# ConvFFN up: two plain pairs of blocks in the place of three, and the second half's residual rows issued behind the factor sums

## The chip, the cores and the metric

The kernel runs on one core of a Trainium2 chip. The metric is the device time of one execution in microseconds; the kernel before has a median of 817.88 us over three runs. Engines are named as in the profile: PE (TensorE, the matrix engine), PEld (its weight loads), DVE (VectorE), ACT (ScalarE), POOL (GpSimd) and SP (SyncE, which here only issues DMAs).

## What is computed

A decoder block over 512 tokens of 1024 channels: two causal token mixers, a gated merge, a residual and LayerNorm, then a ConvFFN with another residual and LayerNorm. The change touches the seam between the first LayerNorm and the first half of the ConvFFN:

```python
mix = mixed @ w_out[l]
x = layer_norm(ALPHA * x + mix, ln1_g[l], ln1_b[l])

z = x @ w_ffn_in[l]                       # 1024 -> 2 x 2816
u, gv = jnp.split(z, [D_FF], axis=-1)
u = causal_dwconv(u, w_ffn_dw[l], b_ffn_dw[l])
y_ffn = (jax.nn.gelu(u) * gv) @ w_ffn_out[l]
x = layer_norm(ALPHA * x + y_ffn, ln2_g[l], ln2_b[l])
```

## The kernel before

Every product of matrices is made of three matmuls: each operand is split into a high part, rounded by a cast on ACT, and a low part, the rest, by a subtraction on DVE (`split`, L166). `mm3` (L173) then adds high by high, high by low and low by high in PSUM.

ConvFFN up has 22 pairs of blocks, j = 0 to 21. A pair is a block of 128 columns of u and the matching block of the gate branch. It is computed in one of two ways.

A plain pair is two blocks, each over the whole depth of 8 slices of 128. The first `NF` pairs are plain and run together in `up` (L996): first all their blocks for the first half of the tokens (256), then all for the second half. So PE has work while the second half of the tokens is still in LayerNorm 1. `up` calls `pump` ahead of every second slice of the depth. Each call takes one entry from `steps`: an empty step, or a call that traces the transposes and activations of one token block for one half of the depth (`ln1_transposes`, L927). `SP` (L17) gives the number of empty steps ahead of each of the four token blocks: 9 for block 2, 3 for block 3.

A seven-product pair (`seven`, L690) is a 2 x 2 block product done with seven products of half the depth and half the tokens in the place of eight. It needs sums of the weights (`weight_sums`, L659: loads two tiles d and e, forms t13 and t24, and splits b21, then b11 with b22, t1 with t3, t2 with t4) and sums of the activations (`factor_sums`, L940: for each of two token blocks of a half four sums, each one split; most are made in place, on top of an input). Its first product is b11 by a11 into the bank X, then b21 by a12 into W, t1 by s1 into Z, then t2 by s2 into X again. The seventh is left to the following pair (`finish`).

Tiles of the same tag share memory: a new tile waits until the old one's last reader is done. The weights' high and low parts take turns in two rings of five tiles (tags hi and lo). `ring_pair` (L648) places every fifth pair elsewhere, in two extra tiles, where the caller gives some:

```python
if more is not None and ring_n[0] % 5 == 4:
    out.append(p1p.tile([P, 1024], F32R, tag=more, name=f"s{tag}_{key}"))
```

The gates call it 8 x 3 times without extra tiles, so the count is 24 at the first seven-product pair. For ConvFFN up the extra tags are oh2 and oh3. The same tags hold x1[2] and x1[3], the normalised rows of token blocks 2 and 3 (L896). `residual` (L892) multiplies such rows by gamma and adds beta on DVE, in place, and stores them through SP's queue; they are loaded again for the second LayerNorm. For blocks 2 and 3 these calls are collected in `late` and traced when j is `NF`, right after `prepare` of that pair.

The order of instructions on each engine is decided when the program is built: a planner goes by the order in which the code traces them and by when it expects each to be ready. An instruction that is ready early can so be issued ahead of ones that were traced before it. `tc.issue_after(i)` forces what is traced inside it, as far as it is on i's engine, to be issued behind i.

Of the kernel before, what the change touches and what calls it, by code (L numbers as in the profile page):

```python
# [10 lines left out]
F32R = mybir.dt.float32r  # L11
BF16 = mybir.dt.bfloat16
WARM = 7
PLAIN = 3
NF = 3
PLAINS = tuple(range(PLAIN))
SP = (6, 0, 9, 3)  # L17
I32 = mybir.dt.int32
AF = mybir.ActivationFunctionType
ALU = mybir.AluOpType  # L20
# [48 lines left out]
def hybrid_block(ctx: ExitStack, tc: tile.TileContext, wts: bass.AP, xT_d: bass.AP,  # L69
# [3 lines left out]
    ve, ac, po, pe = nc.vector, nc.scalar, nc.gpsimd, nc.tensor  # L73
# [25 lines left out]
    def limit(i):  # L99
        return min(e for e in (W_G, W_FI + 2 * PLAIN, W_S) if e > i) - 1  # L100

# [58 lines left out]
    def weight(i):  # L160
        while state[0] <= min(i + AHEAD, limit(i)):
            fetch(state[0])
            state[0] += 1
        return loaded.pop(i)

    def split(hi, lo, src, hi_eng=None, lo_eng=None):  # L166
        if hi_eng is None:
            ac.copy(hi, src)  # L168
        else:
            hi_eng.tensor_copy(hi, src)  # L170
        (lo_eng or ve).tensor_tensor(lo, src, hi, ALU.subtract)  # L171

    def mm3(ps, a, b, start, stop, more=False):  # L173

# [213 lines left out]
    def cln_channels(j):  # L388
        ps = bank(7 if j else 6)
        for tb in range(NT):  # L390
            pe.transpose(ps[:, tb * P:tb * P + P], cn[tb][:, j * P:j * P + P], ident)
        g, b = pcol(PC_CG + j), pcol(PC_CBETA + j)
        sg = tmp.tile([P, T], F32, tag="t0", name=f"cls{j}", bufs=3)
        y = tmp.tile([P, T], F32, tag="t1", name=f"cly{j}")
        ac.activation(sg, ps, AF.Sigmoid, bias=b, scale=g)  # L395
        ac.activation(y, ps, AF.Identity, bias=b, scale=g)  # L396
        ve.tensor_tensor(y, y, sg, ALU.mult)
        split(ch[:, j], cl[:, j], y)
# [432 lines left out]
    def fo_sums(n, behind):  # L831

        fo = lambda t, m: wts[W_FO + FO_OF[t] + m]
        c, m = divmod(n, 4)
        t, b, a = (("t1", "b12", fo("b11", m)), ("t2", "b22", tsum["t1"][m]), ("t3", "b12", fo("b22", m)),
                   ("t4", "b21", tsum["t2"][m]))[c]

        po.dma_start(tsum[t][m][0:1, 0:16], behind[0:1, 0:16])
        po.dma_start(tsum[t][m], fo(b, m))
        po.dma_start(tsum[t][m], a, accum_op=ALU.add, max_dma_last_dim=4096)  # L840
# [20 lines left out]
    for m in range(NH, KD):  # L861
# [5 lines left out]
        t = tmp.tile([P, T], F32, tag="t0", name=f"gm{m}", bufs=3)  # L867
# [55 lines left out]

    keep = {}
    late = []

    def ln1_transposes(half, tb, n):  # L927
        pt = bank(obk[half][2 * (tb % 2) + n])
        for k in range(4):
            pe.transpose(pt[:, k * P:k * P + P], x1[tb][:, (4 * n + k) * P:(4 * n + k + 1) * P], ident)  # L930
        t = tmp.tile([P, T], F32, tag=("kt", "kT")[n] if half == 0 else ("tot", "t1")[n], name=f"a{half}{n}_{tb}")

        for k in range(4):
            ks = slice(k * P, k * P + P)
            ac.activation(t[:, ks], pt[:, ks], AF.Identity, bias=pcol(PC_L1B + 4 * n + k), scale=pcol(PC_L1G + 4 * n + k))
        dst = (slice(None), half, slice(4 * n, 4 * n + 4), slice((tb % 2) * P, (tb % 2) * P + P))
        split(x1h[dst], x1l[dst], t.rearrange("p (k t) -> p k t", k=4))
        keep[half, n, tb % 2] = t

    def factor_sums(i, sh, sl):  # L940

        a11, a12, a21, a22 = keep[0, 0, i], keep[0, 1, i], keep[1, 0, i], keep[1, 1, i]
        dst = lambda t, n: t[n][:, :, i * P:i * P + P]
        four = lambda t: t.rearrange("p (k t) -> p k t", k=4)

        def emit(n, t):
            split(dst(sh, n), dst(sl, n), four(t))
        ve.tensor_tensor(a22, a21, a22, ALU.add)
        emit(0, a22)
        ve.tensor_tensor(a22, a22, a11, ALU.subtract)  # L950
        emit(1, a22)
        ve.tensor_tensor(a11, a21, a11, ALU.subtract)
        emit(2, a11)
        ve.tensor_tensor(a12, a12, a22, ALU.subtract)
        emit(3, a12)
# [27 lines left out]
    def hid(part):  # L983

        for tag, c0, n in ([("ch", 0, 4), ("cl", 4, 4)], [(f"sc{i}", 8 + 2 * i, 2) for i in range(4)])[part]:
            t_ = p1p.tile([P, n, T], F32, tag=tag, name=f"hT{tag}")
            for c in range(n):
                hT[c0 + c] = t_[:, c]
            for c in range(0, n, 2):
                hT2.append(t_[:, c:c + 2])  # L990
        for c in range(16, NFF) if part else ():
            hT[c] = tmp.tile([P, T], F32, tag=("tot", "kt", "gg")[(c - 16) // 2], name=f"hT{c}")
# [3 lines left out]
    def up(ws, halves):  # L996
        pss = [cring.get() for _ in ws]
        for hf in halves:
            for ps, w in zip(pss, ws):
                for k in range(KD):  # L1000
                    if k % 2 == 0:
                        pump()
                    ks = slice(k * P, k * P + P)
                    if hf is None:
                        dst, x = ps.rearrange("p (a t) -> p a t", a=2), (x1h[:, :, k], x1l[:, :, k])
                    else:
                        dst, x = ps[:, hf * 256:hf * 256 + 256], (x1h[:, hf, k], x1l[:, hf, k])
                    mm3(dst, (w[0][:, ks], w[1][:, ks]), x, k == 0, k == KD - 1)
            while steps:
                pump()  # L1010
        return pss

    def act(j, u, g):
        a = tmp.tile([P, T], F32, tag="t0", name=f"fa{j}", bufs=3)
        w = [pcol(PC_FW + 3 * j + i) for i in range(3)]
        ac.activation(a, u, AF.Identity, bias=pcol(PC_FB + j), scale=w[2])
        ve.scalar_tensor_tensor(a[:, 1:], u[:, 0:T - 1], w[1], a[:, 1:], ALU.mult, ALU.add)
        ve.scalar_tensor_tensor(a[:, 2:], u[:, 0:T - 2], w[0], a[:, 2:], ALU.mult, ALU.add)
        ac.activation(a, a, AF.Gelu_apprx_tanh)
        ve.tensor_tensor(hT[j], a, g, ALU.mult)  # L1020

    def seven_up(j, w, sh, sl):

        a11, a12, a22 = [(x1h[:, h, 4 * n:4 * n + 4], x1l[:, h, 4 * n:4 * n + 4]) for h, n in ((0, 0), (0, 1), (1, 1))]
        pc = tmp.tile([P, 3, 256], F32, tag="mv", name=f"pc{j}", bufs=1)
        ug = tmp.tile([P, 2, T], F32, tag="qq", name=f"ug{j}")

        def last(X):
            urgent(ac.copy, ug[:, 0, 256:512], X)
            act(j, ug[:, 0], ug[:, 1])  # L1030
        seven(cring, 5, w, (a11, a12, a22), list(zip(sh, sl)), pc, ug, last)

    def prepare(j):
        i = W_FI + 2 * j
        if j in PLAINS:
            if state[0] <= i:
                assert state[0] == i
                fetch(i)
                fetch(i + 1)
                state[0] += 2  # L1040
            return [loaded.pop(i), loaded.pop(i + 1)]
        t = [p1p.tile([P, 1024], F32, tag=tag, name=f"T{tag}_{j}") for tag in ("oh0", "oh1")]
        b21 = [tmp.tile([P, T], F32R, tag=tag, name=f"b{tag}_{j}") for tag in ("kT", "t1")]
        return weight_sums(i, t, b21, ("oh2", "oh3"))

    resident[W_FI + 2 * NF - 2] = lambda: tuple(p1p.tile([P, 1024], F32R, tag=f"sc{i}", name=f"fir{i}") for i in range(2))
    fir = p1p.tile([P, 2, 1024], F32R, tag="cl", name="fir")
    resident[W_FI + 2 * NF - 1] = lambda: (fir[:, 0], fir[:, 1])
    first = [weight(W_FI + i) for i in range(2 * NF)]
    pss = up(first, (0, 1))  # L1050
    sht = p1p.tile([P, 4, 4, 256], F32R, tag="ol", name="sh")
    sh = [sht[:, n] for n in range(4)]
    sl = [p1p.tile([P, 4, 256], F32R, tag=f"sv{n}", name=f"sl{n}") for n in range(4)]
    for i in range(2):
        factor_sums(i, sh, sl)
    hid(0)
    for j in range(NF):
        act(j, *pss[2 * j:2 * j + 2])
    assert state[0] == W_FI + 2 * PLAIN, state

    for j in range(NF, NFF):
        if NF + 1 <= j <= NF + 12:
            fo_sums(j - NF + 3, hT[j - 2])
        if j == NF:
            w = prepare(j)
            for f in late:
                f()
            hid(1)
        wn = prepare(j + 1) if j + 1 < NFF else None
        if j in PLAINS:  # L1070
            if pending:
                pending.pop()()
            act(j, *[up([t], (None,))[0] for t in w])
        else:
            seven_up(j, w, sh, sl)
        w = wn
# [23 lines left out]
    four = lambda *tags: [lambda k, t=t: p1p.tile([P, 2, 2, 256], F32R, tag=t, name=f"so{t}_{k}") for t in tags]  # L1100
# [54 lines left out]
    for n, t in enumerate(FOP):  # L1155
        nxt = None
        load_rest(n, ops[0][0][:, 0, 0:1])
        for m in range(4):
# [3 lines left out]
            for c in range(2):  # L1162
                first, end = m == 0 and c == 0, m == 3 and c == 1
                for i in range(2):
# [7 lines left out]
                    hi, lo = (o[:, c, i * P:i * P + P] for o in ops[m])  # L1172
# [114 lines left out]
```

## Time and profile before

| | us |
|---|---|
| median of 3 runs (817.06 to 818.1) | 817.88 |
| the profiled execution | 817.08 |
| its span, first to last instruction | 815.2 |
| PE busy | 803.5 |
| DVE busy | 654.1 |
| ACT busy | 478.5 |

The profiled execution's own time is 1.9 us longer than its span; a difference in the span is taken as the same difference in the time. A busy share is a mean over the whole kernel. What counts here is the seam between 469 and 530 us, where PE goes from the W_out product through the plain pairs to the seven-product pairs, and there the rows of single instructions say more than the shares. Matmuls overlap, so the cost of one is the distance between two starts and not its duration; on DVE too the next instruction starts a little ahead of the listed end of the one before.

### The profile page before, as it was taken

To read this page: it belongs to the slowest core of one execution; us is meant where nothing else is said; L and a number is where in the kernel's file an instruction comes from. 1 tells how busy PE (TensorE), PEld (TensorE's weight loads), DVE (VectorE), ACT (ScalarE), POOL (GpSimd) and SP (SyncE) were. 2 spreads that over 40 slices of the span, in tenths; PEclk is the share of its full clock that TensorE was granted. 3 is DMA by queue.
4 is the path that set the end of the run, shared out by engine and by line. 5 is a ranking of instruction groups with operands and counts; after the bars stand their busy time and mean duration, and the time that the engine had idled before them with its cause. 6 is when DMAs were issued, how large, how long until landed. Compare 5 with 4: busy or idle time off the path is not lost.

```text
span 815.2 us, 14709 instructions
## 1 busy us (share of the span) xinstructions
PE 803.5 (99%) x5723; PEld 711.6 (87%) x5723; DVE 654.1 (80%) x1158; ACT 478.5 (59%) x856; POOL 111.0 (14%) x194
## 2 busy tenths in 40 slices
PE   9999999999999999999999999999999999999995
PEld 6888778888888788999988899999999999888884
DVE  5598687888877649788474899899898999999566
ACT  5356657576779865566741657466666666776400
POOL 0012331333323200001200000011111100000000
PEclk9999999999999999999999999999999999999998
DMA  8569876756545663466885322467676753777502
GB/s 305 173 142 246 205 162 149 184 130 155 140 121 133 141 180 114 115 175 171 199 281 227 107 100 80 136 181 203 181 205 194 192 161 116 253 238 229 171 26 78
DMA packets 38534, 136.50 MB, mean 167 GB/s; under 512 B 4928, under 2 KB 5824, under 8 KB 38208
## 3 DMA queue, kind: packets, MB, share of 16 engines
q1 hardware_dynamic: 27072, 90.98, 33.2%
q0 software_dynamic: 9952, 40.90, 24.4%
q10 hardware_dynamic: 1440, 3.68, 1.2%
q8 instruction: 45, 0.74, 0.4%
q14 instruction: 25, 0.20, 0.1%
HBM read 108.28 MB, written 20.97 MB: 159 GB/s over the span
## 4 chain that ended last, share of the span: by engine, by line
PE 96%; ACT 1%; DVE 1%; DMA 0%; issue 0%; DVEq 0%
PE ps L175 30%; PE ps L177 30%; PE ps L176 30%; PE ps L443 1%; PE ps L599 1%; PE ps L588 1%; PE ps L561 1%; PE ps L601 1%; PE ps L615 1%; PE ps L930 0%; PE ps L578 0%; DMA xr<-in_xT 0%; ACT cls L395 0%; ACT cly L396 0%; PE ps L379 0%; DVE x1a L1211 0%
## 5 line engine op out<-in xcount | busy, mean ns | idle before, releaser
L175 PE MATMUL ps<-xh,wh 128*128 128x512 f32 x256 | 102.7, 402 | 0.3 <-ACT xh L168 0.3
L177 PE MATMUL ps<-xh,wl 128*128 128x512 f32 x256 | 100.1, 391 | 0.0
L176 PE MATMUL ps<-xl,wh 128*128 128x512 f32 x256 | 99.9, 390 | 0.0
L302 DVE SCALAR_TENSOR_TENSOR cws<-cws,par 128x512 f32<-128x512 f32 x120 | 86.3, 761 | 1.0
L156 ACT CAST wh<-wr 128x1024 fp32r<-128x1024 f32 (+1 forms) x50 | 50.4, 1013 | 57.2 <-PE ps L177 38.5
L157 DVE TENSOR_TENSOR wl<-wr,wh 128x1024 fp32r<-128x1024 f32 (+1 forms) x51 | 58.9, 1162 | 20.0 <-ACT wh L156 19.5
L143 ACT CAST wh<-wr 128x1024 fp32r<-128x1024 f32 x44 | 46.3, 1053 | 41.9 <-PE ps L176 34.2
L175 PE MATMUL ps<-sh,shi_t 128*128 128x256 f32 x228 | 64.5, 283 | 0.0
L176 PE MATMUL ps<-sl,shi_t 128*128 128x256 f32 x228 | 64.5, 283 | 0.0
L177 PE MATMUL ps<-sh,slo_t 128*128 128x256 f32 x228 | 64.5, 283 | 0.0
L175 PEld LDWEIGHTS ps<-xh,wh 128*128 128x128 f32 x256 | 48.1, 188 | 11.1 <-ACT xh L168 1.2
L145 POOL DMA_DIRECT2D wl<-wr x44 | 38.5, 882 | 137.3 <-ACT wl L144 95.5
L177 PEld LDWEIGHTS ps<-xh,wl 128*128 128x128 f32 x256 | 48.0, 188 | 10.3
L171 DVE TENSOR_TENSOR slo_t<-Toh,shi_t 128x1024 fp32r<-128x1024 f32 x38 | 46.5, 1223 | 12.7 <-ACT shi_t L168 12.7
L176 PEld LDWEIGHTS ps<-xl,wh 128*128 128x128 f32 x256 | 48.2, 188 | 9.5 <-DVE xl L171 0.4
L168 ACT CAST shi_t<-Toh 128x1024 fp32r<-128x1024 f32 x38 | 39.5, 1047 | 14.8 <-PE ps L176 13.0
L144 ACT ACTIVATE wl<-wh 128x1024 fp32r<-128x1024 f32 x44 | 46.5, 1059 | 0.5
L293 ACT COPY pc<-ps 128x256 f32<-128x256 f32 x57 | 21.2, 372 | 41.7 <-PE ps L177 41.2
L175 PEld LDWEIGHTS ps<-sh,shi_t 128*128 128x128 f32 x228 | 43.8, 192 | 0.0
L176 PEld LDWEIGHTS ps<-sl,shi_t 128*128 128x128 f32 x228 | 43.8, 192 | 0.0
L177 PEld LDWEIGHTS ps<-sh,slo_t 128*128 128x128 f32 x228 | 43.8, 192 | 0.0
L171 DVE TENSOR_TENSOR slo_b<-wr,shi_b 128x1024 fp32r<-128x1024 f32 x27 | 33.0, 1223 | 2.4 <-ACT shi_b L168 2.4
(465 smaller groups left out, 2574.5 us busy)
## 6 DMA issues: line engine op xcount, KB each, us to landing
wr<-in_wts SPq DMA_DIRECT2D x137, 512.0 KB, 4.3
wl<-wr POOLq DMA_DIRECT2D x44, 512.0 KB, 5.1
t<-in_wts POOLq DMA_DIRECT2D x24, 512.0 KB, 4.9
wr<-t SPq DMA_DIRECT2D x16, 512.0 KB, 4.2
t<-t POOLq DMA_DIRECT2D x8, 512.0 KB, 6.8
x<-in_x ACTq DMA_DIRECT2D x4, 512.0 KB, 9.5
x_d<-x SPq DMA_DIRECT2D x4, 512.0 KB, 2.8
x1a<-x_d SPq DMA_DIRECT2D x4, 512.0 KB, 3.6
```

The costliest lines, as they stand in the source:

```text
L143: ac.copy(hi, raw)
L144: ac.mul(lo, hi, -1.0)
L145: po.dma_start(lo, raw, accum_op=ALU.add)
L156: ac.copy(hi[:, c], raw[:, c])
L157: ve.tensor_tensor(lo[:, c], raw[:, c], hi[:, c], ALU.subtract)
L168: ac.copy(hi, src)
L171: (lo_eng or ve).tensor_tensor(lo, src, hi, ALU.subtract)
L175: pe.matmul(ps, a[0], b[0], start=start, stop=False, skip_group_check=more)
L176: pe.matmul(ps, a[0], b[1], start=False, stop=False, skip_group_check=more)
L177: pe.matmul(ps, a[1], b[0], start=False, stop=stop, skip_group_check=more)
L293: f(*args)
L302: ve.scalar_tensor_tensor(cacc[j], cpad[j][:, i:i + T], w, cacc[j], ALU.mult, ALU.add)
```

## The change

`PLAIN` and `NF` go from 3 to 2. Pairs 0 and 1 are plain and run together in `up`, so four blocks and not six; pair 2 is computed by seven products, and its weights are packed for that in DRAM. The tiles apart from the ring that held the weights of pair 2 now hold those of pair 1. `SP` stays as it is.

`split` returns its subtraction, and `factor_sums` keeps the last one in `made`. The residual rows of token blocks 2 and 3 are traced at the same place as before, but their DVE operations are to be issued behind the last subtraction of the factor sums.

```diff
--- before.py
+++ after.py
@@ -11,8 +11,8 @@
 F32R = mybir.dt.float32r
 BF16 = mybir.dt.bfloat16
 WARM = 7
-PLAIN = 3
-NF = 3
+PLAIN = 2
+NF = 2
 PLAINS = tuple(range(PLAIN))
 SP = (6, 0, 9, 3)
 I32 = mybir.dt.int32
@@ -168,7 +168,7 @@
             ac.copy(hi, src)
         else:
             hi_eng.tensor_copy(hi, src)
-        (lo_eng or ve).tensor_tensor(lo, src, hi, ALU.subtract)
+        return (lo_eng or ve).tensor_tensor(lo, src, hi, ALU.subtract)
 
     def mm3(ps, a, b, start, stop, more=False):
 
@@ -923,6 +923,7 @@
 
     keep = {}
     late = []
+    made = []
 
     def ln1_transposes(half, tb, n):
         pt = bank(obk[half][2 * (tb % 2) + n])
@@ -944,7 +945,7 @@
         four = lambda t: t.rearrange("p (k t) -> p k t", k=4)
 
         def emit(n, t):
-            split(dst(sh, n), dst(sl, n), four(t))
+            made[:] = [split(dst(sh, n), dst(sl, n), four(t))]
         ve.tensor_tensor(a22, a21, a22, ALU.add)
         emit(0, a22)
         ve.tensor_tensor(a22, a22, a11, ALU.subtract)
@@ -1063,8 +1064,10 @@
             fo_sums(j - NF + 3, hT[j - 2])
         if j == NF:
             w = prepare(j)
-            for f in late:
-                f()
+
+            with tc.issue_after(made[0].ins):
+                for f in late:
+                    f()
             hid(1)
         wn = prepare(j + 1) if j + 1 < NFF else None
         if j in PLAINS:
```

## Rows read from the trace of the kernel before

**Rows 1.** The page's busy time of each engine (busy us, share of the span, instructions), and below it the view of what PE waited for over the whole execution (engine, line, tile, releaser: us in total, times, longest).
```profile
PE 803.5 (99%) x5723; PEld 711.6 (87%) x5723; DVE 654.1 (80%) x1158; ACT 478.5 (59%) x856; POOL 111.0 (14%) x194
...
PE ps L615 <- ACT cly L396: 1.3, 1, 1.3
PE ps L113 <- DVE wrs L109: 1.2, 1, 1.2
PE ps L175 <- ACT xh L168: 0.3, 1, 0.3
```

**Rows 2.** PE's timeline through ConvFFN up (start in us, duration in us, line, operation, out<-in, how many were merged): the first matmul on the normalised activations, the transposes of token blocks 2 and 3, the first matmul of the fifth plain block, the first matmul of the second half of the tokens, and the first product of three seven-product pairs in a row.
```profile
469.46 0.28 PE L175 MATMUL ps<-x1h,wh 128*128 128x256 f32 x1
...
477.74 1.03 PE L930 MATMUL ps<-ident,x 128*128 128x128 f32 x8
...
480.40 0.60 PE L930 MATMUL ps<-ident,x 128*128 128x128 f32 x4
...
481.56 0.60 PE L930 MATMUL ps<-ident,x 128*128 128x128 f32 x4
...
482.71 0.28 PE L175 MATMUL ps<-x1h,fir 128*128 128x256 f32 x1
...
488.47 0.28 PE L175 MATMUL ps<-x1h,wh 128*128 128x256 f32 x1
...
505.75 0.28 PE L175 MATMUL ps<-x1h,shi_b 128*128 128x256 f32 x1
...
514.39 0.28 PE L175 MATMUL ps<-x1h,shi_b 128*128 128x256 f32 x1
...
524.47 0.28 PE L175 MATMUL ps<-x1h,shi_b 128*128 128x256 f32 x1
```

**Rows 3.** DVE's timeline in the same stretch, same columns: three pieces of weight work inside the LayerNorm chain, the residual rows of blocks 2 and 3 (L893, L894), two of the x1l subtractions, the first operation of the factor sums, the subtraction for the first seven-product pair's b11 and b22, and the last subtraction of the factor sums.
```profile
473.69 1.17 DVE L157 TENSOR_TENSOR fir<-wr,fir 128x1024 fp32r<-128x1024 f32 x1
...
474.91 0.68 DVE L681 TENSOR_TENSOR Toh<-wr,Toh 128x512 f32<-128x512 f32 x1
...
475.65 0.68 DVE L682 TENSOR_TENSOR Toh<-wr,Toh 128x512 f32<-128x512 f32 x1
...
478.95 1.22 DVE L893 TENSOR_TENSOR x<-x,gb 128x1024 f32<-128x1024 f32 x1
...
481.83 1.22 DVE L894 TENSOR_TENSOR x<-x,gb 128x1024 f32<-128x1024 f32 x1
...
483.56 1.22 DVE L893 TENSOR_TENSOR x<-x,gb 128x1024 f32<-128x1024 f32 x1
484.70 0.69 DVE L171 TENSOR_TENSOR x1l<-a,x1h 128x512 fp32r<-128x512 f32 x1
485.30 0.69 DVE L948 TENSOR_TENSOR a<-a,a 128x512 f32<-128x512 f32 x1
485.90 1.22 DVE L894 TENSOR_TENSOR x<-x,gb 128x1024 f32<-128x1024 f32 x1
487.04 0.69 DVE L171 TENSOR_TENSOR x1l<-a,x1h 128x512 fp32r<-128x512 f32 x1
...
493.18 1.22 DVE L171 TENSOR_TENSOR slo_b<-wr,shi_b 128x1024 fp32r<-128x1024 f32 x1
...
499.24 0.69 DVE L171 TENSOR_TENSOR sl<-a,sh 128x512 fp32r<-128x512 f32 x1
```

**Rows 4.** ACT's timeline, same columns (in brackets: idle time before and what released it): the first activation of token block 2, the casts of block 3's halves of the depth, and the cast of b11 and b22.
```profile
478.37 1.85 ACT L935 ACTIVATE a<-ps,par 128x128 f32<-128x128 f32 x5 [7.67 <-PE ps L930]
...
483.88 0.68 ACT L168 CAST x1h<-a 128x512 fp32r<-128x512 f32 x1
...
485.65 0.62 ACT L168 CAST x1h<-a 128x512 fp32r<-128x512 f32 x1
...
486.70 1.04 ACT L168 CAST shi_b<-wr 128x1024 fp32r<-128x1024 f32 x1
```

**Rows 5.** Busy time by stretch (from:to in us, length, then busy us and instructions of PE, PEld, DVE, ACT, POOL, then PE's granted clock, the DMA engines' share, GB/s): the stretch around the first seven-product pair, ten pairs behind it, and two stretches at the kernel's tail.
```profile
478.90:513.00 34.10, 34.10 (x287) 34.10 (x287) 34.07 (x47) 25.50 (x46) 1.05 (x2) 1.00 0.28 93
...
515.80:616.00 100.20, 100.20 (x837) 100.20 (x836) 90.10 (x117) 62.05 (x99) 14.44 (x24) 1.00 0.68 184
...
805.00:810.00 5.00, 1.37 (x7) 0.79 (x5) 3.54 (x10) 0.00 (x0) 0.00 (x0) 1.00 0.21 80
810.00:815.00 5.00, 0.00 (x0) 0.00 (x0) 2.02 (x6) 0.00 (x0) 0.00 (x0) 0.54 0.27 105
```

**Rows 6.** SP's timeline (the issues of DMAs) in the same stretch, merged: the stores of blocks 2 and 3 and the next weight loads. Below it, of the view of the store's line, the time from issue to landing of its four stores.
```profile
483.07 4.41 SPq L895 DMA_DIRECT2D x_d<-x  x2
494.50 5.23 SPq L666 DMA_DIRECT2D wr<-in_wts  x2
...
DMA to landing us min/median/max: 2.6/2.8/3.2
```

**Rows 7.** The last matmul on the first pair's b22 in PE's timeline, and in ACT's timeline the cast that comes behind it.
```profile
512.83 0.28 PE L177 MATMUL ps<-sh,slo_b 128*128 128x256 f32 x1
...
513.03 1.05 ACT L168 CAST shi_t<-Toh 128x1024 fp32r<-128x1024 f32 x1 [0.95 <-DVE soat_b L171]
```

## The prediction

> **What bounds the kernel now.** I read the page's busy shares first, then what TensorE (PE) waited for. PE is busy 803.5 of 815.2 us, and its waits sum to under 3 us, all outside ConvFFN up [rows 1]. So a saved matmul is saved time, as long as nothing new makes PE wait. Next I read PE's timeline over the stage that is changed, for its rate and its boundaries [rows 2]: the second half of the W_out product ends at 469.46, the six plain blocks (three pairs, first half of the tokens) run to 488.47, their second half to 505.75, and there the first pair by seven products starts. From 482.71 to 488.47 is 5.76 us for 48 matmuls, so a matmul of 256 columns costs 0.12 us. The seven-product pairs repeat at the same rate: first product at 514.39, the next pair's at 524.47, 10.08 us = 84 x 0.12. Then VectorE (DVE) and ScalarE (ACT) in the same stretch [rows 3, 4]: after PE has finished W_out, the last two token blocks still go through LayerNorm 1, transposes, four ACT passes each, a cast and a subtraction. Last, busy times by stretch [rows 5]: DVE is busy 34.07 of 34.10 us between 478.9 and 513.0, and 90.1 of 100.2 in the pairs after. PE hides all that, but only just in this stretch.
>
> **What the change saves.** A plain pair in halves is 2 blocks x 8 x 3 x 2 = 96 matmuls, 96 x 0.12 = 11.52 us; by seven products it is 7 x 4 x 3 = 84, 10.08 us. Sum: -1.44 us of PE. Everything else of the pair is on other engines. Two subtractions of plain weights (1.17 to 1.22 us each) go from DVE; one full-width and two half-width sums, three full-width subtractions, a half-width one and two sums of products come, some 8.1 us busy for 2.4, so +5.7 us of DVE. Over the later pairs that is hidden in DVE's idle tenth [rows 5]; if it were not, it would cost at most those 5.7 us. The GpSimd sums for the down projection begin one pair earlier and wait for hT[1] in the place of hT[2]; GpSimd is busy 111 of 815 us [rows 1], cost nothing.
>
> **First gap: the second half of the plain blocks.** A matmul of that half needs the activations of token blocks 2 and 3 together. With four plain blocks, the first half is 96 matmuls and the 16 transposes among them, and it ends where block five begins today: 482.71 [rows 2]. The last input for k = 0 to 3 is the cast that starts at 483.88 and lasts 0.68, and the subtraction behind it, which takes 0.69 [rows 3, 4]. Without the residual rows ahead of it on DVE that subtraction runs at 484.6 to 485.2. Today blocks five and six are the cover: the half starts at 488.47, with everything ready at 487.7. Now PE stands from 482.8 to about 485.2: +2.4 us. Moving the residual rows can't shorten this much, since ACT's chain from 478.37 to 486.27 is without a break [rows 4]. Lower bound 0.1: DVE does three pieces of weight work inside the LayerNorm chain (473.69, 474.91, 475.65; 2.3 us together [rows 3]), and if the new order puts them elsewhere the chain ends so much sooner. Upper bound 3.6: with fewer plain weights a ring slot is free early, so one more subtraction of weights (1.2 us) can slip into that chain. I take 2.4, since the same three pieces are due in the same place. Once n = 0 is there, its 48 matmuls (5.76 us) cover the other half of the depth, which ACT finishes at 486.3.
>
> **Second gap: the first seven-product pair.** Its first operand pair (b11 with b22) doesn't lie in the ring but in tiles oh2 and oh3: ring_pair takes the extra tags when its count is 4 modulo 5, and the gates leave it at 24. Those tiles hold x1[2] and x1[3], the rows that the late residual writes and stores. So cast and subtraction of b wait for the two stores. Today the residual rows run at 478.95 to 487.0 as filler [rows 3], the stores issue at 483.07 and 487.2 and land in 2.8 us [rows 6], the cast of b is at 486.70 and its subtraction at 493.18, 11 us before its use at 505.75. That the extra tiles really gate is seen one turn later: the cast that takes them next stands at 513.03, right behind the last matmul on the first b at 512.83 [rows 7].
>
> The change puts all four residual operations behind the last subtraction of the factor sums. Today that one starts at 499.24. Without three residual operations and the 1.2 us for b between them, I put its end at 497.5; bounds 495.4 (some 15 operations at the pitch of 0.60 us between the starts at 484.70, 485.30 and 485.90 [rows 3], behind ACT's last cast at 486.3, nothing between) and 499.9 (as today). Then: four operations at the pitch of 1.14 between 483.56 and 484.70, 4.6; the activation of the second plain pair, traced ahead of them, comes between for 0 to 2.0; the store's landing 2.8 [rows 6]; the subtraction 1.2. So b is whole 8.6 to 10.6 us after the sums; I take 9.0: at 506.5, bounds 504.0 to 510.5.
>
> PE by then: the second half ends at 485.2 + 11.5 = 496.7. Then the two products that need no b (b21 by a12, t1 by s1, 24 matmuls) last to 499.6. From there X can't go on: its first product is b11. The next pair can: its b lies in the ring, and its first three products are another 36 matmuls, 4.3 us, to 503.9; the fourth needs t2, whose ring turn is the same extra tiles. So the gap is 506.5 - 503.9 = 2.6 us if the issue order brings the next pair forward, and 506.5 - 499.6 = 6.9 if not; bounds 0 and 10.9. PE's order here is decided when the program is built, by what is expected to be ready: the first transposes of block 2 stand behind 69 matmuls of the plain blocks, at 477.74, where the code emits them ahead of the 55th (nine empty steps of six matmuls) [rows 2]. So I take the reordered case, 2.6.
> The Trainium skill (TensorE: Matmul & The Clock Gate, section "Step-by-step: what each phase is for") says that the engine pulls weight loads ahead but that matmuls stay in program order. By that a wait for b would hold all behind it, and the sum would be the 6.9; the row shows that the order written may already differ from the code's, so I give that less weight.
>
> **Queues behind the moved step.** Behind the residual rows on DVE stand the weights of the next pair; DVE is full here, so they come as PE's spare products need them, and that is inside the bound. On SP's queue the two stores move from 483 and 487 to some 500 and 503. Behind them are the loads for the pair after next, which wait for the subtraction of b anyway (today at 494.50, right behind 493.18 [rows 3, 6]); at 507 + 3.5 us they still land some 9 us before that pair starts at about 520. Cost nothing; if that cover is gone, the pair waits for the difference.
>
> **The sum.** -1.44 + 2.4 + 2.6 = +3.6 us on the profiled execution: 817.08 + 3.6 = 820.7. That execution lies 0.8 below the median of the runs, 817.88, so the median should come out at 821.5.
>
> **Rivals.**
> First, and on the other side, no gap at all: with the residual rows gone from the front of DVE's queue and the three fillers out of the LayerNorm chain, what PE needs comes before PE does. It decides from the point where the last x1l subtraction for k = 0 to 3 ends by 482.8 in place of 485.2, and b is whole by 499.6, which the fill by the next pair can put off to 503.9. For it: 4.6 us less on DVE ahead of the sums. Against: ACT's unbroken chain. -1.44 gives 816.4.
> Second, the first gap alone: the second is covered because the sums end at 495.4 and no activation comes between. Total +1.0, with the filler +2.2: 818.9 to 820.1.
> Third, slower by more: the order keeps first_x of the first seven-product pair in its place, and all of PE waits for the stores. It decides from the point where the planner expects b before it expects the next pair's operands. -1.44 + 2.4 + 6.9 = +7.9, 825.8. For it: DVE has no free time to prepare the next pair. Against: the displaced transposes [rows 2].
> Fourth, the change doesn't do what it says: the residual rows would have come behind the sums anyway. Against: today they stand ahead of the sums [rows 3].
> The clock is no rival for the first gap: in the tail, a stretch with PE idle for 3.6 us still has the granted clock at 1.00, the 2.4 GHz level, and it is the next stretch that shows 0.54 [rows 5].
>
> **How the numbers follow.** Forecast (both gaps, next pair brought forward; +1.6 to +5.5) 0.45; first gap alone 0.20; no bringing forward 0.20; no gap 0.12; the rest 0.03. Likeliest time 821.5. About 0.2%, 1.6 us, is what a measurement of this kernel can tell from no change. Faster by that (below 816.2): the lower part of the no-gap case and of the rest, 0.08. Within it (816.2 to 819.5): the other part of the no-gap case, half of the first-gap case, the edge of the forecast, 0.25. Slower: 0.67. The range from 816.4 to 826.0 leaves out about half of the case without bringing forward and a part of the no-gap case.
>
> **What would show it.** In the changed profile: PE's waits list a gap of 2 to 3 us ahead of the first matmul on the second half, released by the x1h cast or the x1l subtraction; both residual stores after the sums' last subtraction; cast and subtraction of the first b behind those stores; and a second PE wait on that subtraction, with products of the next pair before it. The pairs after repeat at 10.08 us. The prediction is wrong if PE has no idle time between 480 and 510, if b is prepared before the sums end, or if DVE falls behind for many pairs, which would show as waits on slo_t far beyond 520.

## The result, and the profile after

| | us | ratio to before |
|---|---|---|
| before, median of 4 runs (817.06 to 818.73) | 817.99 | |
| after, median of 4 runs (827.75 to 830.03) | 829.09 | 1.0137 [1.0124, 1.015] |
| predicted | 821.5 (816.4 to 826.0) | |

The change costs 11 us where some 4 were forecast, and the time lies outside the range. The profiled execution of after took 830.03 us, 12.95 more than that of before.

Read first, on the page of after, the busy times (engine, busy us, share, instructions).
```profile
PE 808.1 (98%) x5711; PEld 714.3 (86%) x5711; DVE 659.6 (80%) x1165; ACT 481.6 (58%) x862; POOL 111.2 (13%) x194
```
Then the view of what PE waited for in after (engine, line, tile, releaser: us in total, times, longest). bkT and bt are the tiles of b21's high and low part, shi_b and slo_b those of b11 with b22, shi_t and slo_t those of the t operands; pc holds copies of finished products.
```profile
PE ps L175 <- ACT x1h L168: 1.8, 1, 1.8
PE ps L177 <- DVE bt L171: 1.8, 1, 1.8
PE ps L175 <- ACT shi_b L168: 1.4, 1, 1.4
...
PE ps L175 <- ACT shi_t L168: 1.1, 1, 1.1
PE ps L175 <- ACT pc L293: 1.0, 1, 1.0
PE ps L177 <- DVE slo_b L171: 0.8, 1, 0.8
```
PE has 12 matmuls less than in [rows 1], which is 12 x 0.12 = 1.44 us, and yet is busy 4.6 us longer. So besides the six new waits, 7.9 us together, there are matmuls that became slower. DVE has 5.5 us more of work; 5.7 were worked out.

PE's timeline of after shows where (start, duration, operation, how many merged, in brackets the wait and its releaser): the transposes of block 3, the last first-half matmul before the gap, the first of the second half, two later ones, the first of the first seven-product pair, and the first after each wait.
```profile
482.00 1.09 PE L931 MATMUL ps<-ident,x 128*128 128x128 f32 x8 [0.17 <-DVE x L884]
...
483.05 0.28 PE L177 MATMUL ps<-x1h,fir 128*128 128x256 f32 x1
485.11 0.95 PE L175 MATMUL ps<-x1h,wh 128*128 128x256 f32 x3 [1.78 <-ACT x1h L168]
...
486.07 0.41 PE L176 MATMUL ps<-x1l,wh 128*128 128x256 f32 x1
486.28 0.41 PE L177 MATMUL ps<-x1h,wl 128*128 128x256 f32 x1
...
498.22 0.28 PE L175 MATMUL ps<-x1h,bkT 128*128 128x256 f32 x1
...
500.86 0.39 PE L177 MATMUL ps<-x1h,bt 128*128 128x256 f32 x1 [1.76 <-DVE bt L171]
501.08 0.28 PE L175 MATMUL ps<-x1h,bkT 128*128 128x256 f32 x1
...
506.21 0.58 PE L175 MATMUL ps<-x1h,shi_b 128*128 128x256 f32 x1 [1.41 <-ACT shi_b L168]
...
514.56 0.39 PE L177 MATMUL ps<-x1h,slo_b 128*128 128x256 f32 x1 [0.83 <-DVE slo_b L171]
...
522.60 0.38 PE L175 MATMUL ps<-sh,shi_t 128*128 128x256 f32 x1 [1.05 <-ACT shi_t L168]
```
Two places lose time. At the boundary of the halves the first half ends at 483.17, 0.4 late, since block 3's rows came later; PE then stands to 485.11 (1.94); and the 96 matmuls of the second half take 498.22 - 485.11 = 13.11 us in the place of 11.52 (1.59). Together 3.9 us. The seam behind it is not one gap: from 498.22 to 554.54, where the wait for pc ends, there are 384 matmuls, 46.1 us of work in 56.3, so 10.2 us are lost, in five waits (6.05 us with pc's) and in slow matmuls around them. With the 1.44 saved, 3.9 + 10.2 - 1.4 = 12.7 of the 12.95 us are placed.

The slow matmuls are seen in the pitch, 486.28 - 486.07 = 0.21 us where it was 0.12, and in the busy times by stretch of after (columns PE, PEld, DVE, ACT, POOL busy, then the granted clock, the DMA share and GB/s).
```profile
482.80:485.30 2.50, 0.72 (x6) 0.52 (x5) 1.85 (x4) 2.50 (x8) 0.00 (x0) 0.98 0.00 0
485.30:500.00 14.70, 13.79 (x102) 13.59 (x102) 12.90 (x21) 11.86 (x20) 0.00 (x0) 0.89 0.00 1
500.00:505.00 5.00, 3.94 (x22) 3.65 (x22) 5.00 (x7) 1.63 (x4) 0.53 (x1) 0.73 0.33 105
505.00:510.00 5.00, 3.79 (x21) 3.79 (x22) 5.00 (x6) 2.21 (x3) 0.52 (x1) 0.59 0.90 269
510.00:515.00 5.00, 4.17 (x35) 3.96 (x34) 3.49 (x4) 0.62 (x1) 0.85 (x1) 1.00 0.93 303
```
The granted clock falls behind the wait that ends at 485.11 and again behind the one that ends at 500.86, to means of 0.89, 0.73 and 0.59, that is to the 1.2 GHz level for a part of each stretch. Behind the three shorter waits from 514.56 on it stays at 1.00. Before it was 1.00 throughout [rows 5].

DVE's timeline of after, the pieces that answer to [rows 3] (slo_t, slo_b, bt and L670 are weights of seven-product pairs, L884 the normalised rows of block 3, L1018 an activation of the plain pairs, L893 and L894 the residual rows):
```profile
477.67 1.22 DVE L171 TENSOR_TENSOR slo_t<-Toh,shi_t 128x1024 fp32r<-128x1024 f32 x1
...
479.27 1.23 DVE L670 TENSOR_TENSOR Toh<-wr,wr 128x1024 f32<-128x1024 f32 x1 [0.19 <-DMA wr<-in_wts]
...
481.14 0.81 DVE L884 TENSOR_SCALAR x<-x,lmva,lrsa 128x1024 f32<-128x1024 f32 x1
...
495.58 2.00 DVE L171 TENSOR_TENSOR sl<-a,sh 128x512 fp32r<-128x512 f32 x3
497.49 1.40 DVE L1018 SCALAR_TENSOR_TENSOR fa<-ps,par,fa 128x511 f32<-128x511 f32 x2
...
500.12 0.68 DVE L171 TENSOR_TENSOR bt<-wr,bkT 128x512 fp32r<-128x512 f32 x1
500.72 1.22 DVE L893 TENSOR_TENSOR x<-x,gb 128x1024 f32<-128x1024 f32 x1
...
505.92 1.22 DVE L894 TENSOR_TENSOR x<-x,gb 128x1024 f32<-128x1024 f32 x1
507.06 1.22 DVE L171 TENSOR_TENSOR slo_b<-wr,shi_b 128x1024 fp32r<-128x1024 f32 x1
...
509.33 1.22 DVE L171 TENSOR_TENSOR slo_b<-wr,shi_b 128x1024 fp32r<-128x1024 f32 x1
...
513.28 1.23 DVE L171 TENSOR_TENSOR slo_b<-wr,shi_b 128x1024 fp32r<-128x1024 f32 x1
```
The sums end at 497.58. Work on the activations of both plain pairs follows, then the low part of the first pair's b21 (500.12), and the residual rows run among other work from 500.72 to 507.14. Only then come weights of the pairs that PE was to go on with, the first slo_b at 507.06. The first pair's own b is whole at 513.28 + 1.23 = 514.51, and PE's matmul at 514.56 waits for it. ACT's timeline has the cast ahead of that subtraction ("issue": the profile shows nothing that released it):
```profile
508.16 1.05 ACT L168 CAST shi_b<-wr 128x1024 fp32r<-128x1024 f32 x1 [2.00 <-issue]
```

SP's DMA issues of after, which answer to [rows 6] (issue, duration; merged ones have the time from first to last):
```profile
504.30 0.33 SPq L895 DMA_DIRECT2D x_d<-x  x1
...
507.17 0.33 SPq L895 DMA_DIRECT2D x_d<-x  x1
508.31 25.85 SPq L666 DMA_DIRECT2D wr<-in_wts  x6
```
And the view of DMA issues of after from 500 to 520 us (KB each, median us to landing):
```profile
wr<-in_wts SPq DMA_DIRECT2D x4, 512.0 KB, 5.6
x_d<-x SPq DMA_DIRECT2D x2, 512.0 KB, 4.9
```
Of the view of the store's line in after, the time from issue to landing of its four stores:
```profile
DMA to landing us min/median/max: 2.6/3.2/6.0
```
Stores and weight loads now fall together: DMA share 0.90 and 0.93 in the two stretches above (0.28 in [rows 5]), and both land in some 5 us where a store took 2.8 [rows 6]. The two late stores take 3.8 and 6.0 us, so they land at 508.1 and 513.2. The first pair's b is cast at 508.16 and subtracted at 513.28, each right behind a landing: that is the gate of oh2 and oh3.

### The profile page after: what moved, and what is told of

It is laid out like the page before. It is cut to its first block, busy times and chain, and to the rows that moved or that the text cites. A ratio compares the mean times of both kernels' runs of the same rounds, so it can differ in the third digit from the quotient of the medians.

```text
span 828.2 us, 14694 instructions
## 1 busy us (share of the span) xinstructions
PE 808.1 (98%) x5711; PEld 714.3 (86%) x5711; DVE 659.6 (80%) x1165; ACT 481.6 (58%) x862; POOL 111.2 (13%) x194
## 4 chain that ended last, share of the span: by engine, by line
PE 87%; DVE 5%; DMA 4%; ACT 3%; issue 1%; DVEq 0%; ACTq 0%
PE ps L175 28%; PE ps L176 27%; PE ps L177 27%; DMA wr<-in_wts 3%; PE ps L443 1%; PE ps L599 1%; PE ps L588 1%; PE ps L561 1%; ACT shi_t L168 1%; DVE Toh L670 1%; PE ps L601 1%; PE ps L615 1%; PE ps L578 0%; DMA xr<-in_xT 0%; DVE sl L171 0%
## 5 line engine op out<-in xcount | busy, mean ns | idle before, releaser
L175 PE MATMUL ps<-sh,shi_t 128*128 128x256 f32 x240 | 68.8, 287 | 1.1 <-ACT shi_t L168 1.1
L176 PE MATMUL ps<-sl,shi_t 128*128 128x256 f32 x240 | 68.4, 285 | 0.0
L177 PE MATMUL ps<-sh,slo_t 128*128 128x256 f32 x240 | 68.3, 285 | 0.0
L171 DVE TENSOR_TENSOR slo_t<-Toh,shi_t 128x1024 fp32r<-128x1024 f32 x40 | 48.9, 1222 | 12.6 <-ACT shi_t L168 12.5
L168 ACT CAST shi_t<-Toh 128x1024 fp32r<-128x1024 f32 x40 | 41.6, 1049 | 19.8 <-PE ps L176 11.5
L175 PEld LDWEIGHTS ps<-sh,shi_t 128*128 128x128 f32 x240 | 46.6, 194 | 1.5 <-ACT shi_t L168 1.3
L176 PEld LDWEIGHTS ps<-sl,shi_t 128*128 128x128 f32 x240 | 46.6, 194 | 0.0
L177 PEld LDWEIGHTS ps<-sh,slo_t 128*128 128x128 f32 x240 | 46.5, 194 | 0.0
```

The source lines that it names most:

```text
L171: return (lo_eng or ve).tensor_tensor(lo, src, hi, ALU.subtract)
L175: pe.matmul(ps, a[0], b[0], start=start, stop=False, skip_group_check=more)
L176: pe.matmul(ps, a[0], b[1], start=False, stop=False, skip_group_check=more)
L177: pe.matmul(ps, a[1], b[0], start=False, stop=stop, skip_group_check=more)
```

## The experiments

Two theories of the seam. **Gates (G)**: the tiles hold PE up (b in oh2 and oh3, which x1[2] and x1[3] hold until their stores have landed; b21 in kT and t1, which the activations hold until the sums have read them). **DVE's order (D)**: the residual rows stand on a full DVE ahead of the weights that PE wants next, whichever tiles those use. Each ratio is against the kernel before on the same chip; "up" is the length of the stage in the profiled execution, which can lie up to 2.5 us from the median of its runs, from the first matmul on x1h and wh to the first of the down projection: 226.37 us before, 239.25 after.

**1. Each half of the change alone.** Two plain pairs, with the rows in their old place:
```diff
-PLAIN = 3
-NF = 3
+PLAIN = 2
+NF = 2
```


> Only the two constants are changed; the residual rows stay free to be issued early. Theory G (gates): the loss has three parts, the lost cover ahead of the second half with the slow clock behind it (about 4 us of excess at 483 to 489 in the changed kernel), the first seven-product pair's b waiting for tiles oh2 and oh3, and weights of the next pairs that come late. The first part stays here: 4 - 1.4, so at least 820.5. As far as the rows of block 3 still end late, the others stay too, and the time comes out between 823 and 829. Theory R (the moved rows are the loss): without the move only the first part is left, 820 to 821.

And three plain pairs, with the rows behind the sums:
```diff
-            for f in late:
-                f()
+            with tc.issue_after(made[0].ins):
+                for f in late:
+                    f()
```


> Three plain pairs as before, and only the residual rows behind the factor sums. Theory G: two more plain blocks are 11.5 us more of PE work ahead of the first b, so the delay of b is covered: 817.5 to 819. Theory R: the moved rows delay b and the weight loads behind it by themselves: 822 to 827.

Two plain pairs alone: 823.29 us, ratio 1.0066 [1.0054, 1.0078], up 231.87. Late rows alone: 818.66 us, 1.0012 [1.0003, 1.0021], up 227.31, and no PE wait in the stage. Both lie where G put them. So the pairs alone cost 5.4 us, the rows alone 1.0, both 11.2: 4.8 us come from their meeting. With three plain pairs PE has 11.5 us more of work (96 matmuls) ahead of the first product by seven, and the same late rows are nearly covered.

**2. The first b in the ring.** The change whole, with the ring's count moved by one, so that the extra tiles fall to t1 with t3 of the next pair:
```diff
     first = [weight(W_FI + i) for i in range(2 * NF)]
+    ring_n[0] += 1
```


> The changed kernel, with the count of ring_pair raised by one, so that b11 and b22 of the first seven-product pair lie in the ring and not in oh2 and oh3; the work is the same. Theory G: the gate on the first b is gone; the first gap stays (about 4 us), the excess behind 498 (10.4 us) falls by half or more: 820 to 824. Rival D (DVE has simply too much to do here, whatever the order): no difference that matters, 827 to 830.

826.0 us, 1.0092 [1.0077, 1.0106]: between the two theories. The gap of b is gone, and the first gap nearly too (x1h wait 0.31). But PE still waits 1.9 us for bt, and 4.7 us for pc in three later places.

**3. PE kept busy in the first gap.** Twelve matmuls whose results nobody uses, between the halves:
```diff
+            if hf == 1:
+                for i in range(12):
+                    pe.matmul(pss[3][:, 256:512], ws[3][0][:, 0:P], x1h[:, 0, i % KD], start=True, stop=True)
```


> The changed kernel with 12 matmuls that nothing uses (1.4 us of PE work, overwritten by the real ones) between the two halves of the plain blocks, where PE stands idle 1.8 us. Theory C (the idle time makes the granted clock fall, and the 15 matmuls behind it at half speed cost 1.6 us of the 4): the granted clock stays at 1.00 from 483 to 489 and the time falls by 1 to 1.6, to 827.5. Rival: the clock is not set by this gap, the time is as the changed kernel's, 829, or up to 0.5 longer.

828.85 us, 1.014 [1.0122, 1.0157]. The busy times of this run over the boundary (columns as above, the granted clock third from the end):
```profile
482.80:489.00 6.20, 5.85 (x47) 5.45 (x46) 4.67 (x9) 4.82 (x12) 0.00 (x0) 1.00 0.00 0
```
The clock stays at 1.00, so in this place it is the idle time that lets it fall. The time doesn't gain, as the rival said: the wait for bt now ends at 500.14 in the place of 500.86, and that for slo_b at 514.10 in the place of 514.56. PE comes earlier to gates that open when DVE is ready.

**4. The rows on GpSimd.** Two plain pairs, the rows of blocks 2 and 3 on GpSimd; the same with the ring's count moved; and the same in the kernel before:
```diff
-        ve.tensor_tensor(x1[tb], x1[tb], gb1[0], ALU.mult)
-        ve.tensor_tensor(x1[tb], x1[tb], gb1[1], ALU.add)
+        en = po if tb >= 2 else ve
+        en.tensor_tensor(x1[tb], x1[tb], gb1[0], ALU.mult)
+        en.tensor_tensor(x1[tb], x1[tb], gb1[1], ALU.add)
```


> Two plain pairs, the residual rows of blocks 2 and 3 neither moved nor on DVE but on GpSimd (the same two operations). Theory D (behind 498 the loss is DVE's load: 4.6 us of residual rows fall into a stretch where it is full): the excess behind the first gap, 2.0 us with the rows early on DVE, goes to under 1, and the 0.8 us wait for x1l in the first gap goes too: 820.5 to 822. Rival (the rows' DVE time is not what counts): as with two plain pairs alone, 823.3.

> As the run with the rows on GpSimd, and b11 and b22 of the first seven-product pair in the ring, so that its first product (12 matmuls) fills the first gap. If the loss is the first gap plus what the late rows do: gap filled to about 1 us, nothing behind it, 817.5 to 819. Rival S (the six pairs after the seam have too little lead whatever the rows do, as with b in the ring and late rows): 9 us of waits behind 498 stay, 824 to 826.

> The kernel before (three plain pairs) with the residual rows of blocks 2 and 3 on GpSimd, as a control. PE waits for nothing in that stretch, so DVE's relief gives nothing: 817.5 to 818.5. If it is faster by over 1 us, DVE's load costs time in the kernel before too.

828.9 us, 1.0136 [1.0122, 1.0149]; 826.94, 1.0123 [1.0105, 1.0141]; and in the kernel before 820.83, 1.0043 [1.003, 1.0057]. All three lie above what was expected. Taking the rows off DVE costs time in all three, for a reason that neither theory had. DVE's timeline in the last of these:
```profile
479.11 3.42 DVE L670 TENSOR_TENSOR Toh<-wr,wr 128x1024 f32<-128x1024 f32 x1
482.45 5.71 DVE L171 TENSOR_TENSOR x1l<-a,x1h 128x512 fp32r<-128x512 f32 x2
```
GpSimd's timeline in the same run (L894 and L895 are there the multiplication and the addition of a row):
```profile
479.02 2.42 POOL L894 TENSOR_TENSOR x<-x,gb 128x1024 f32<-128x1024 f32 x1 [73.23 <-PE ps L931]
481.52 3.27 POOL L895 TENSOR_TENSOR x<-x,gb 128x1024 f32<-128x1024 f32 x1
```
While GpSimd works on a row, a DVE operation takes 2.9 to 3.4 us in the place of 0.69 and 1.22, so nothing is taken off DVE. These runs say nothing between G and D.

**5. Gates opened one after the other, the rows in their old place.** Two plain pairs and the ring's count moved, as in 2; then also b21 of the first seven-product pair in a tag that is free by then:
```diff
-        b21 = [tmp.tile([P, T], F32R, tag=tag, name=f"b{tag}_{j}") for tag in ("kT", "t1")]
+        b21 = [tmp.tile([P, T], F32R, tag=tag, name=f"b{tag}_{j}") for tag in (("gg", "gg") if j == NF else ("kT", "t1"))]
```


> Two plain pairs, rows early on DVE, b in the ring: the run with b in the ring without the moved rows. If the moved rows cause the 9 us of waits behind 498 that b in the ring left: at most 2 us of them stay, 818 to 820. Rival S (too little lead): 824 to 826.

> Two plain pairs, rows early on DVE, b in the ring as in the run with ring and early rows, and b21 of the first seven-product pair in the free tag gg, not in kT and t1, which hold inputs of the factor sums. If the wait for bt at 500 (2.2 us) is those two tags' gate, it goes, and b21's product helps to fill the first gap: 1.4 less than the kernel before plus at most 0.7 of gaps, 816.2 to 817.3. Rival D (DVE is full, the wait comes back at the next operand): 819 to 820.5.

The first: 820.36 us, 1.0035 [1.0022, 1.0048], up 228.13; it lies just above the range for the moved rows as the cause, and far below rival S. The second: 817.19 us, 0.9998 [0.999, 1.0007], up 225.98, and one PE wait of 0.2 us in the stage. PE's timeline of the first:
```profile
482.71 0.28 PE L175 MATMUL ps<-x1h,shi_b 128*128 128x256 f32 x1
...
484.62 0.62 PE L175 MATMUL ps<-x1h,wh 128*128 128x256 f32 x3 [0.31 <-ACT x1h L168]
...
499.50 0.39 PE L177 MATMUL ps<-x1h,bt 128*128 128x256 f32 x1 [2.05 <-DVE bt L171]
```
With b in the ring, PE puts the first product of pair 2 (shi_b; 12 matmuls on the first half's tokens) into the first gap, and 0.31 us is left of the 2.0 and 0.8 us that the run with two plain pairs alone waits there (for x1h and x1l). What remains is the wait for b21's low part, 2.05 us, and with b21 elsewhere that is gone too. So without the moved rows the gates are the whole cost of the two plain pairs that can be measured: +5.4, +2.9, -0.2 us as they are opened.

**6. Gates opened, the rows behind the sums.** The change whole, with no extra tiles until the ring has made 30 pairs of tiles, so that the first use of them falls into the fourth seven-product pair; then also b21 in gg; and the last of these again with the rows in their old place:
```diff
-            if more is not None and ring_n[0] % 5 == 4:
+            if more is not None and ring_n[0] > 30 and ring_n[0] % 5 == 4:
```


> The changed kernel (rows behind the sums) with no extra tiles used until the fifth seven-product pair, so that nothing that those pairs need waits for x1[2] and x1[3]; all five pairs' operands take turns in the ring. Theory G (what the moved rows cost is the tiles that they hold): the waits behind 498 shrink to the one for bt, 2 us, and the time is 819.5 to 822. Rival D (the rows' 4.6 us on DVE come at the worst time, in front of the next pairs' weights): 824 to 827, as with b alone in the ring.

> As the run without extra tiles, and b21 of the first seven-product pair in gg. Theory G: no gate of the seam is left, 816.5 to 818.5. Rival D: 823 to 826, the rows still stand in front of the next pairs' weights.

> The kernel with two plain pairs, no extra tiles for the first seven-product pairs' weights and b21 of the first such pair in the tag gg, as in the run before it, but with the residual rows of blocks 2 and 3 left in their old place. The whole output is computed. Theory D (the place of the moved rows on DVE, ahead of the weights of the next pairs, costs some 4.6 us by itself): without the move 816.5 to 818 us, no PE wait over 0.5 us after 495 us, up 226 to 227 us long. Rival (keeping the extra tiles out is itself what costs, since the ring then turns with one pair fewer): 821 to 822.5 us with the same waits for pc near 543 us.

825.66 us, 1.0092 [1.0074, 1.011]; 821.82, 1.0046 [1.0034, 1.0058], up 230.12; and with the rows in their old place 817.78, 1.0006 [0.9993, 1.0019], up 226.30. The first lies where D put it, with the same ratio as with b alone in the ring (experiment 2), so the extra tiles' hold on the next pair's t1 cost nothing there that can be measured. The second lies between the two ranges. The last two differ only in the place of the rows, and with them of their stores, with neither gate in either: the ratios are 0.0040 apart, 3.3 us with an uncertainty of some 1.4, and "up" 3.8. So the rows' place has a price without the gates, as D says; that the shorter ring is itself the cost is out. DVE's timelines, first with the rows late:
```profile
481.66 0.69 DVE L171 TENSOR_TENSOR x1l<-a,x1h 128x512 fp32r<-128x512 f32 x1 [0.60 <-ACT x1h L168]
...
483.58 0.69 DVE L171 TENSOR_TENSOR x1l<-a,x1h 128x512 fp32r<-128x512 f32 x1 [1.23 <-ACT x1h L168]
...
485.49 0.69 DVE L171 TENSOR_TENSOR x1l<-a,x1h 128x512 fp32r<-128x512 f32 x1 [0.49 <-ACT x1h L168]
487.34 0.69 DVE L171 TENSOR_TENSOR sl<-a,sh 128x512 fp32r<-128x512 f32 x1 [1.15 <-ACT sh L168]
...
508.02 1.21 DVE L171 TENSOR_TENSOR slo_b<-wr,shi_b 128x1024 fp32r<-128x1024 f32 x1
```
then with the rows in their old place:
```profile
479.18 1.22 DVE L893 TENSOR_TENSOR x<-x,gb 128x1024 f32<-128x1024 f32 x1
...
486.13 1.22 DVE L894 TENSOR_TENSOR x<-x,gb 128x1024 f32<-128x1024 f32 x1
...
503.90 1.22 DVE L171 TENSOR_TENSOR slo_b<-wr,shi_b 128x1024 fp32r<-128x1024 f32 x1
```
Early, the four rows fill the time in which DVE would wait for ACT's casts. Late, that time stands empty (0.60 + 1.23 + 0.49 + 1.15 = 3.5 us of waits), and the same slo_b comes at 508.02 in the place of 503.90; the stage began 0.67 us later in that run (470.35 against 469.68), so it is 3.45 us later. What the rows leave idle on DVE, 3.5 us, is about what the kernel loses. PE loses it in three waits, of 0.60, 0.28 and 1.88 us, and in shorter pauses. The longest comes late in the stage, in PE's timeline with the rows late:
```profile
543.54 0.39 PE L175 MATMUL ps<-sh,shi_t 128*128 128x256 f32 x1 [1.88 <-ACT pc L293]
```
ACT copies that pc at 543.12, behind an activation that waited for DVE until 541.35 and a cast that waited for a weight load until 542.60. So how much of the 3.3 us is DVE's lateness and how much the loads that come later with it stays open.

## Why the prediction went wrong, step by step

Three steps failed: the first gap was costed without the clock, the second gap with too short a way to the first b and with a b21 taken as ready, and the rows' new place on DVE was put at nothing. In their place the runs show 3.9 us for the first gap, 10.2 for the seam behind it, and 3.3 for the rows' place, measured by itself with no gate left.

**Saving, -1.44: right.** PE has 12 matmuls less. With all gates open the stage is 0.4 us shorter than before (225.98 against 226.37), the rest of the 1.44 going into pauses of under 0.4 us; none of the versions is faster than the kernel before by what can be measured.

**First gap, +2.4: right in kind, 3.9 in size.** PE waited for the x1h cast as said, until 485.11 where 485.2 was estimated. Its wait of 1.8 us is in the bounds; the term lacked the slower clock behind the wait, 1.59 us over the 96 matmuls, and 0.4 us for weights (477.67, 479.27) that now stand ahead of block 3's rows, which is the filler of the upper bound. The sentence that failed is "the clock is no rival for the first gap": it rested on a row of the tail [rows 5], in which the clock still stood at 1.00 in the stretch with the idle time, and fell in the next. That the next stretch fell was the part that mattered. The run with PE kept busy shows that the idle time brought the fall here; it also shows that these 1.5 us don't reach the end, since the gates behind them hardly move.

**The cover that was missed.** The prediction listed the first pair's products that need no b, as a filling for the second gap, and not that b11 by a11 (and b21 by a12) needs only the first half's tokens. Were b there at 482.7, that product would fill the first gap; the runs with b in the ring show it, x1h's wait falling to 0.31. So the extra tiles made both gaps, not only the second.

**Second gap, +2.6: the right gate, and not the only one.** b did wait behind the rows and their stores, and next pairs were brought forward. But b was whole at 514.5, not 506.5, outside the bounds (504.0 to 510.5). The sums ended at 497.58, as estimated (497.5). From there the first row came after 3.1 us and not after at most 2.0, the four rows took 6.4 us with other work between and not 4.6, and the second store 6.0 to land and not 2.8. Four things were not foreseen.
- The two products "that need no b" were taken as ready. Their b21 lies in tiles that the activations hold, so its low part stood behind the sums and two activations, at 500.12: PE's wait of 1.76 us. With gg in its place it vanishes (2.05 to none, and 3.0 us of time, the ratio falling from 1.0035 to 0.9998).
- PE stood at 498.94 before that one low part, though the matmul behind it, bkT at 501.08, had its operands. So here nothing passes within the program's order: the planner's reordering seen in [rows 2] fills only what it foresaw. The Trainium skill (TensorE: Matmul & The Clock Gate, section "Step-by-step: what each phase is for") says that matmuls stay in program order, and this row agrees.
- Pairs 3 and 4 were both brought forward, and their weights came on DVE, ACT and the DMAs ahead of the first pair's b: slo_b at 507.06 and 509.33 are theirs, that of 513.28 is the first pair's. The DMA share reached 0.93, and a weight load took 5.6 us to land.
- The clock fell there as well, to means of 0.73 and 0.59.

**Queues, "cost nothing": wrong.** The prediction named the weights behind the rows on DVE and said that they come as PE's spare products need them. The runs show 3.3 us for the rows' place with no gate at all. In the change as it is, gates and place act together: by the ratios, the rows' late place costs 5.8 us with the gates shut (1.0137 against 1.0066), 4.7 with b in the ring (1.0092 against 1.0035) and 3.3 with all open (1.0046 against 1.0006). With three plain pairs it is 1.0. The stores' move on SP's queue was also said to be free; how much of the loss the bunched loads make by themselves no run took apart.

**DVE's +5.7 in the idle tenth: right.** 5.5 us of work came, and the version with the gates open and the rows early carries as much (DVE busy 659.1 us against 654.1) without being slower. But the seam doesn't have the tenth: DVE was busy 34.07 of 34.10 us there [rows 5], as the prediction itself read, and in the run with the rows late and the gates open it is busy without a break from 500 to 520 us, so work that is moved within the seam finds no free time behind.

**The sum and the range.** 3.9 in the place of 2.4 and 10.2 in the place of 2.6 make +12.7. The bound of 10.9 for the second gap was written down and not taken into the range, whose upper end, 826.0, came from the rival of 6.9. The rival "no gap", 816.4, is closest to the version with all gates open and the rows early (817.19 against 817.21 before it on the same chip, so none of the 1.44 shows), but not by its reason: the cast for k = 0 to 3 starts no earlier there (484.00 against 483.88 [rows 4]), PE has other work in the gap.

## What to carry to other kernels

A step that is used as filler can have a price of zero where it stands and not elsewhere: before moving it, look for the waits that it covers on its own engine. Here the kernel lost about what they came to. When a stage that covers late operands is made shorter, list for every tile of the next stage what held that memory before, low parts and rarely noticed temporaries included, and give each its own release time. And an idle time of PE of some 2 us is to be costed twice, with the clock of the stretch after it falling and without, since the runs show both.

## What was not expected of the hardware

The clock fell to the 1.2 GHz level after a single wait of 1.8 us in an otherwise full stage (pitch from 0.12 to 0.21 us for some 15 matmuls), where in the kernel before the stretch with 3.6 idle us of the tail had shown 1.00 [rows 5]. But not every such wait brings the fall. In the run with b in the ring and the rows early, the stretch behind the wait of 2.05 us has the full clock:
```profile
499.50:505.00 5.50, 5.50 (x46) 5.50 (x47) 5.50 (x8) 2.32 (x5) 0.95 (x2) 1.00 0.30 97
```
The same holds behind a wait of 2.90 us with b in the ring and the rows late, one of 2.67 in the kernel before with the rows on GpSimd, and the one of 1.88 above, while one of 1.48 in the run without extra tiles was followed by a mean of 0.68 (499.6 to 505). So the length of one wait doesn't decide it; what does, these runs don't show.

While a GpSimd operation over two tensors in SBUF runs (2.4 to 3.3 us for 128x1024), a DVE operation over two tensors in SBUF is held until about its end: L670 3.42 us in the place of 1.22, x1l 2.9 in the place of 0.69. The Trainium skill (SBUF — State Buffer, section "SBUF: two separate sides") says that the two engines share a pair of ports, that of a DVE operation with two inputs in SBUF and a GpSimd operation that reads SBUF whichever starts first holds it for its whole instruction, and that the other is blocked. The rows agree: about one DVE operation passes for each of GpSimd's.
